# Reading the moving operand of TensorE products in turns of four columns from two halves, with another distance to the weight blocks

## The chip, the cores and the metric

The kernel runs on one core of a Trainium2 chip. The metric is the device time of one execution in microseconds. Engines are named as in the profile: PE (TensorE matmuls), PEld (its weight loads), DVE (VectorE), ACT (ScalarE), POOL (GpSimd) and SP, whose queue issues the DMAs.

## The reference

It is one inference step of a two-layer backbone with two groups of 128 tokens (context and latent), model width 2048. Both groups go through the same weights:

```python
for l in range(DEPTH):                                   # DEPTH = 2
    mod = silu(cond) @ w_ada[l] + b_ada[l]               # shift, scale, gate, twice
    h = rmsnorm(x, g_norm_mix[l]) * (1 + sc1) + sh1
    m = mixer_ab(h, ...) if l % 2 == 0 else mixer_c(h, ...)
    x = x + gt1 * m
    h = rmsnorm(x, g_norm_ffn[l]) * (1 + sc2) + sh2
    x = x + gt2 * conv_ffn(h, ...)                       # D_FF = 5632
y = rmsnorm(x, g_final)
```

The even layer's mixer holds multi-head latent attention and grouped-query attention; the odd layer's is differential attention. Each has one input projection, attention over the group's own keys (for the latent group also over 128 cached keys), and one output projection. `conv_ffn` projects up to 2 x 5632 features, convolves each over three neighbouring tokens, multiplies silu(gate) by the value and projects down. All inputs are float32. Context tensors (compressed keys and values) are outputs too.

## The kernel before

Activations lie transposed: 128 features on the partitions, tokens along the row, the 128 context tokens first and the 128 latent tokens behind them (NT = 256 columns). A product of an activation with a weight matrix runs over blocks of 128 x 128 weights. To get float32 accuracy from TensorE's faster type (fp32r), both sides are split into a high and a low part: `split` (L215 to L217) has ACT write the high part and DVE the difference. An operand tile thus holds, for each block of 128 features, 256 columns of high parts and 256 of low parts (ROW = 512 columns, 2,048 bytes): `hx` (normalised activations, also the attention output of the even layer), `g` (gated features), `oall` (attention output of the odd layer), `ql` (query latents), and `kv_in`, which has 3 x 128 columns, cached keys in the middle.

For each block, `gemm` (L300) issues three matmuls into one PSUM bank (tile `acc`): high weights with high operand (L309), high weights with low operand (L310), low weights with high operand (L313). Each matmul has its own weight load of 128 columns (512 bytes per partition). `first_three` (L279) does the same for the first three output blocks of a stage, interleaved (L295 to L297). Outputs are read from PSUM by ACT or DVE (residual add, convolution, copies), in token order.

Weights come by DMA from SP's queue, 1 MB at a time, into `raw` (3 buffers), and are split into `wh` and `wl` (4 buffers each, 1,024 columns, eight blocks of 512 bytes). The products of adaLN (`w_ada`) are worked in between: some on PE (L434, plain f32 with 32 weight columns), some on DVE (L419), paced by `pump` with rates per stage. Attention scores and values (L635, L649 to L651, L951, L970 to L972) and transposes (L382, L625, L876, L937, L992) are plain f32 matmuls.

The tile framework orders the instructions with a simulated timeline; only steps marked `keep_in_program_order` are pinned. Stages follow one another: even mixer (to about 497 us of the profile), ConvFFN of layer 0 (497 to 1205), odd mixer (1205 to 1690), ConvFFN of layer 1 (1690 to 2362), final norm.

Where a tile lies in a partition follows from the order of the pools. Small `pad` tiles set the addresses modulo 512: one in the weight pool (L112) and one ahead of the operands in each stage's pool (L659, L910, L1023), the latter sized by `SHIFT`. In the kernel before all operands of these products lie at 96 modulo 512 and all weight blocks at 160, so an operand starts 64 bytes ahead of a block in address (-64, which is SHIFT = 448, modulo 512).

Of the kernel before, what the change touches and what calls it, by code (L numbers as in the profile page):

```python
# [17 lines left out]
P = 128  # L18
D = 2048
KD = D // P  # L20
T = 128
NT = 2 * T
ROW = 2 * NT
SHIFT = 448
NL = 2
GRID_W = 64
EPS = 1e-6
# [56 lines left out]
def step_kernel(ctx: ExitStack, tc: tile.TileContext, A: dict):  # L84
    nc = tc.nc
    pe, dve, act, pool, sp = nc.tensor, nc.vector, nc.scalar, nc.gpsimd, nc.sync

    keep = ctx.enter_context(tc.tile_pool(name="keep", bufs=1))
    wpool = ctx.enter_context(tc.tile_pool(name="wpool", bufs=3))
# [13 lines left out]
    def nm(s):  # L103
        uid[0] += 1
        return f"{s}_{uid[0]}"

    def T_(pl, shape, tag, dt=F32, bufs=None):
        kw = {} if bufs is None else {"bufs": bufs}
        return pl.tile(shape, dt, tag=tag, name=nm(tag), **kw)


    T_(wpool, [P, 48], "pad", bufs=1)  # L112


    cst = T_(keep, [P, NCONST], "cst")
# [70 lines left out]
    def bank():  # L186
        return T_(pmisc, [P, 512], "misc")

    def att_bank():
        return T_(ppool["att"], [P, 512], "att", bufs=3)  # L190
# [30 lines left out]
    class Weights:  # L221
# [29 lines left out]
        def chunk(self):  # L251
# [24 lines left out]
            out, self.blocks = self.blocks[:self.nblk], self.blocks[self.nblk:]  # L276
            return out

    def first_three(W, xh, xl, order, mid=None, fixed=False):  # L279


        pin = tc.keep_in_program_order if fixed else lambda i: i
        raws = [W.load() for _ in range(3)]
        ps = [T_(pacc, [P, 512], "acc") for _ in range(3)]
        blocks = {(c, h): W.halves(raws[c], 8 * h) for c, h in ((0, 0), (1, 0), (2, 0), (0, 1))}
        count = [0] * 3
        for n, (c, k) in enumerate(order):
            if mid and n == len(order) // 2:
                mid()
            if (c, k // 8) not in blocks:  # L290
                blocks[c, k // 8] = W.halves(raws[c], 8)
            wh, wl = blocks[c, k // 8][k % 8]
            a, b = count[c] == 0, count[c] == KD - 1
            count[c] += 1
            pin(pe.matmul(ps[c][:, :NT], wh, xh(k), start=a, stop=False))  # L295
            pin(pe.matmul(ps[c][:, :NT], wh, xl(k), start=False, stop=False))  # L296
            pin(pe.matmul(ps[c][:, :NT], wl, xh(k), start=False, stop=b))  # L297
        return [p[:, :NT] for p in ps]

    def gemm(blocks, xh, xl, n=NT, first=0, between=None):  # L300


        fixed = lambda i: tc.keep_in_program_order(i) if between else i
        ps = T_(pacc, [P, 512], "acc")
        last = len(blocks) - 1
        for i in range(last + 1):
            k = (i + first) % (last + 1)
            wh, wl = blocks[k]
            fixed(pe.matmul(ps[:, :n], wh, xh(k), start=(i == 0), stop=False))  # L309
            fixed(pe.matmul(ps[:, :n], wh, xl(k), start=False, stop=False))  # L310
            if between and i == (last + 1) // 2:
                between()
            fixed(pe.matmul(ps[:, :n], wl, xh(k), start=False, stop=(i == last)))  # L313
        return ps[:, :n]


# [227 lines left out]
    def modulated(st, l, which, W, fixed):  # L544
# [29 lines left out]
        def turn():  # L574
            rest[1](tc.keep_in_program_order)

        ps = first_three(W, lambda k: hx[:, k, :NT], lambda k: hx[:, k, NT:2 * NT],
                         AS_MADE if fixed else IN_TURN, lambda: sum_rows(2, raws[2]), fixed)
        if fixed:
# [75 lines left out]
    def mixer_ab(hx, rb0, st):  # L655
        l = 0
        with tc.tile_pool(name="ab", bufs=1) as ab:
            with tc.tile_pool(name="abp", bufs=1) as pj:
                T_(ab, [P, SHIFT // 4], "pad")  # L659
                kv_in = T_(ab, [P, 4, 2, 3 * T], "kv_in", F32R)  # L660
# [104 lines left out]
                def part(W, k0, n, first, rate, between=None, **kw):  # L765

                    for c in range(23):
                        ps = gemm(W.chunk(), lambda k: hx[:, k0 + k, :NT], lambda k: hx[:, k0 + k, NT:2 * NT])
                        to = pr[:, c] if c < 15 else qb[:, c - 15]
                        if first:  # L770
                            act.copy(to, ps)
                        else:
                            dve.tensor_tensor(out=to, in0=to, in1=ps, op=ALU.add)
                        if between:
                            between(c)
                        pump(rate, **kw)
# [34 lines left out]
            with tc.tile_pool(name="abh", bufs=1) as hp:  # L811
# [35 lines left out]
                for h in range(8):  # L847
                    if h % 2 == 0:
                        for i in range(2):
                            ps = gemm(WQ.chunk(), qh, qlo)  # L850
                            qn[h + i] = T_(hp, [P, NT], "qn", bufs=4)
                            act.copy(qn[h + i], ps)
                            pump(RATE["heads"])
                        ps = gemm(WQ.chunk(), qh, qlo)
                        ev = T_(tmp, [P, NT], "nt", bufs=4)
                        act.copy(ev, ps)
                        qr = T_(hp, [P, NT], "qr", bufs=2)
                        act.copy(qr[:, 0:T], ev[:, 0:T])
                        rope(qr[:, None, T:], ev[:, None, T:], 1, 32, "rcm", "rsm")
                        pump(RATE["heads"])  # L860
# [34 lines left out]
    def mixer_c(cp, hx, W, ready, todo, st):  # L895
# [13 lines left out]
        product = lambda: ready.pop(0) if ready else gemm(W.chunk(), xh, xl, between=todo.pop(0) if todo else None)  # L909
        T_(cp, [P, SHIFT // 4 - 24], "pad")  # L910
        o_all = T_(cp, [P, KD, ROW], "oall", F32R)
# [90 lines left out]
        W = Weights(A["w_out_c"], KD, 1)  # L1002
        oh, ol = (lambda k: o_all[:, k, :NT]), (lambda k: o_all[:, k, NT:2 * NT])
        ready = first_three(W, oh, ol, LAST_LATE)
        for c in range(KD):
            fine[0] = c >= KD - QUIET[2]
# [8 lines left out]
    def ffn(hx, W, ready, todo, l, st):  # L1015
# [4 lines left out]
        with tc.tile_pool(name=f"ffn{l}", bufs=1) as fp, banks(f"pffn{l}") as pf:  # L1020
            feat["home"], feat["pool"] = fp, pf
            feat["due"] = 0.0
            T_(fp, [P, SHIFT // 4], "pad")  # L1023

# [53 lines left out]
    with banks("pab") as ppool["ada"]:  # L1078
# [4 lines left out]
        ps = [bank(), att_bank()]  # L1083
# [168 lines left out]
```

## Time and profile before

| what | value |
|---|---|
| median of two runs | 2388.72 us (2388.01 to 2389.42) |
| profiled execution, first to last instruction (its span) | 2384.0 us; no other time of it is recorded |
| left between span and median | 4.7 us |
| PE busy | 2333.9 us, 98% of the span |
| PEld busy | 2201.5 us, 92% |
| DVE busy | 1775.5 us, 74% |
| ACT busy | 1164.9 us, 49% |
| DMA | 612.94 MB, mean 257 GB/s |
| mean granted TensorE clock | 0.994 |

A matmul in the profile lasts longer than the distance to the next, because matmuls overlap in the array; the busy share of PE is not its pace. The pace is read from the starts, or from the number of matmuls in a stretch. In a group's line the columns are source line, engine, operation, output<-inputs, shapes and count, then busy time and mean duration of one, then the idle time ahead of them and what ended it.

### The profile page before, as it was taken

The numbers are of one execution on the slowest core, as the hardware profiler recorded it, in microseconds if no ns is written. First come the engines' busy times: TensorE is split into PE (matmuls) and PEld (weight loads), VectorE is DVE, ScalarE is ACT, GpSimd is POOL, SyncE is SP. The second block draws the span as 40 slices with busy tenths as digits, with TensorE's granted clock in tenths as the row PEclk, the third lists the DMA queues.
The fourth block names the chain that finished last, engine by engine and source line by source line (L and its number), as shares of the span: only waits on it lengthen the run. The fifth ranks groups of instructions, "written<-read, shape, count | busy, mean of one in ns | idle before, by whom it ended". The sixth has DMA issues, their size and how long they took to land. (4 is left out here: it accounts for less than half of the span.)

```text
span 2384.0 us, 47535 instructions
## 1 busy us (share of the span) xinstructions
PE 2333.9 (98%) x19784; PEld 2201.5 (92%) x19784; DVE 1775.5 (74%) x2720; ACT 1164.9 (49%) x1817; POOL 167.6 (7%) x205
## 2 busy tenths in 40 slices
PE   8999999999999999999999999999999999999997
PEld 6778868789999999999989999998999999999997
DVE  2667545569999999999979777878899855666654
ACT  4345544365554345554455444445655534555542
POOL 0001101100000000001220000023000000000011
PEclk9999999999999999999999999999999999999999
DMA  8886678877777876777766787776767655555553
GB/s 347 352 336 250 226 282 310 317 269 260 261 253 282 296 278 252 265 263 270 297 238 235 277 295 293 257 300 265 257 250 261 212 194 193 193 194 193 194 194 123
DMA packets 92551, 612.94 MB, mean 257 GB/s; under 512 B 9969, under 2 KB 17841, under 8 KB 20529
## 3 DMA queue, kind: packets, MB, share of 16 engines
q1 hardware_dynamic: 92336, 609.91, 69.7%
q8 instruction: 155, 2.54, 0.4%
q14 instruction: 60, 0.48, 0.1%
HBM read 605.12 MB, written 4.75 MB: 256 GB/s over the span
## 5 line engine op out<-in xcount | busy, mean ns | idle before, releaser
L216 ACT CAST wh<-raw 128x1024 fp32r<-128x1024 f32 (+1 forms) x788 | 793.7, 1013 | 963.8 <-PE acc L310 803.0
L217 DVE TENSOR_TENSOR wl<-raw,wh 128x1024 fp32r<-128x1024 f32 (+1 forms) x788 | 921.2, 1182 | 368.9 <-ACT wh L216 363.1
L309 PE MATMUL acc<-hx,wh 128*128 128x256 f32 x4064 | 1132.3, 279 | 10.9 <-ACT wh L216 4.2
L313 PE MATMUL acc<-hx,wl 128*128 128x256 f32 x4064 | 1129.1, 278 | 0.8 <-DVE wl L217 0.8
L310 PE MATMUL acc<-hx,wh 128*128 128x256 f32 x4064 | 1128.3, 278 | 0.0
L309 PEld LDWEIGHTS acc<-hx,wh 128*128 128x128 f32 x4064 | 764.4, 188 | 40.9 <-issue 16.3
L313 PEld LDWEIGHTS acc<-hx,wl 128*128 128x128 f32 x4064 | 764.3, 188 | 11.8 <-issue 8.7
L310 PEld LDWEIGHTS acc<-hx,wh 128*128 128x128 f32 x4064 | 764.9, 188 | 9.4 <-issue 7.9
L310 PE MATMUL acc<-g,wh 128*128 128x256 f32 x1408 | 388.3, 276 | 0.0
L313 PE MATMUL acc<-g,wl 128*128 128x256 f32 x1408 | 388.0, 276 | 0.0
L309 PE MATMUL acc<-g,wh 128*128 128x256 f32 x1408 | 387.8, 276 | 0.0
L419 DVE CUSTOM_DVE_ANT_0 junk<-araw,condb 128x2048 f32<-128x2048 f32 x120 | 274.6, 2289 | 0.0
L310 PEld LDWEIGHTS acc<-g,wh 128*128 128x128 f32 x1408 | 264.3, 188 | 0.0
L313 PEld LDWEIGHTS acc<-g,wl 128*128 128x128 f32 x1408 | 264.1, 188 | 0.0
L309 PEld LDWEIGHTS acc<-g,wh 128*128 128x128 f32 x1408 | 264.0, 188 | 0.0
L172 POOL TENSOR_TENSOR sqacc<-sqacc,sq 128x256 f32<-128x256 f32 x62 | 82.0, 1322 | 1521.7 <-issue 1216.1
L463 DVE SCALAR_TENSOR_TENSOR aacc<-araw,condw,aacc 128x512 f32<-128x512 f32 x150 | 111.3, 767 | 0.2
L586 DVE SCALAR_TENSOR_TENSOR x<-acc,mod,x 128x128 f32<-128x128 f32 x192 | 58.1, 343 | 56.0 <-PE acc L313 55.0
L1030 ACT ACTIVATE cv<-acc,convw 128x256 f32<-128x256 f32 x176 | 98.3, 558 | 1.4 <-PE acc L297 1.4
L434 PE MATMUL ada<-araw,condw 128*32 128x512 f32 x704 | 94.6, 614 | 3.8 <-DMA araw<-w_ada 3.0
L1036 DVE SCALAR_TENSOR_TENSOR cv<-acc,convw,cv 128x254 f32<-128x254 f32 x176 | 84.2, 479 | 3.5
L1033 DVE SCALAR_TENSOR_TENSOR cv<-acc,convw,cv 128x254 f32<-128x254 f32 x176 | 83.5, 475 | 2.6 <-ACT cv L1030 2.5
(236 smaller groups left out, 1893.0 us busy)
## 6 DMA issues: line engine op xcount, KB each, us to landing
araw<-w_ada SPq DMA_DIRECT2D x186, 1024.0 KB, 5.8
raw<-w_up SPq DMA_DIRECT2D x176, 1024.0 KB, 4.8
raw<-w_down SPq DMA_DIRECT2D x88, 1024.0 KB, 4.8
raw<-w_in_c SPq DMA_DIRECT2D x48, 1024.0 KB, 5.3
raw<-w_in_ab SPq DMA_DIRECT2D x19, 1024.0 KB, 7.0
raw<-w_out_ab SPq DMA_DIRECT2D x16, 1024.0 KB, 6.8
raw<-w_out_c SPq DMA_DIRECT2D x16, 1024.0 KB, 4.8
raw<-w_ada SPq DMA_DIRECT2D x6, 1024.0 KB, 9.9
```

The lines of the kernel that those rows point to most:

```text
L172: pool.tensor_tensor(out=st["acc"], in0=st["acc"], in1=sq, op=ALU.add)
L216: pin(act.copy(out_hi, src))
L217: pin(dve.tensor_tensor(out=out_lo, in0=src, in1=out_hi.bitcast(F32), op=ALU.subtract))
L309: fixed(pe.matmul(ps[:, :n], wh, xh(k), start=(i == 0), stop=False))
L310: fixed(pe.matmul(ps[:, :n], wh, xl(k), start=False, stop=False))
L313: fixed(pe.matmul(ps[:, :n], wl, xh(k), start=False, stop=(i == last)))
L419: tc.keep_in_program_order(dve.tensor_tensor_reduce(out=T_(feat["pool"], [P, D], "junk"), in1=feat["row"][:, c], in0=feat["raw"].rearrange ...
L434: i = pe.matmul(ada["ps"][32 * g:32 * g + 32, :], condw[:, 4 * t + g, :], raw[:, g], start=(t == 0), stop=(t == 3), skip_group_check=True)
L463: i = dve.scalar_tensor_tensor(out=acc[:, c], in0=raw[:, g], scalar=condw[:, k, c:c + 1], in1=acc[:, c], op0=ALU.mult, op1=ALU.add)
L1030: pin(act.activation(y, ps, AF.Identity, scale=cw[:, 1, m:m + 1], bias=cw[:, 3, m:m + 1]))
L1033: pin(dve.scalar_tensor_tensor(out=y3[:, :, 1:], in0=p3[:, :, :T - 1], scalar=cw[:, 0, m:m + 1], in1=y3[:, :, 1:], op0=ALU.mult, op1=ALU.add))
L1036: pin(dve.scalar_tensor_tensor(out=y3[:, :, :T - 1], in0=p3[:, :, 1:], scalar=cw[:, 2, m:m + 1], in1=y3[:, :, :T - 1], op0=ALU.mult, op1=A ...
```

## The change

Three edits. A helper `paired` gives a view of a row with 128 x j columns in which the order is: 4 columns of the first 128, 4 columns of the second 128, (4 of the third,) then the next 4 of the first, and so on. All products of `first_three` and `gemm` read their moving operand in that order and write their PSUM tile in the same order, so each result lands where it did. `SHIFT` becomes 256, and the pad in the weight pool grows from 48 to 96 columns: weight blocks move from 160 to 352 modulo 512, operands stay at 96, the distance becomes 256.

```diff
-SHIFT = 448
+SHIFT = 256
+RUN = 4
...
-    T_(wpool, [P, 48], "pad", bufs=1)
+    T_(wpool, [P, 96], "pad", bufs=1)
...
+    def paired(ap):
+
+        return ap.rearrange("p (j i e) -> p i j e", i=T // RUN, e=RUN)
...
-            pin(pe.matmul(ps[c][:, :NT], wh, xh(k), start=a, stop=False))
-            pin(pe.matmul(ps[c][:, :NT], wh, xl(k), start=False, stop=False))
-            pin(pe.matmul(ps[c][:, :NT], wl, xh(k), start=False, stop=b))
+            out = paired(ps[c][:, :NT])
+            pin(pe.matmul(out, wh, paired(xh(k)), start=a, stop=False))
+            pin(pe.matmul(out, wh, paired(xl(k)), start=False, stop=False))
+            pin(pe.matmul(out, wl, paired(xh(k)), start=False, stop=b))
...
         ps = T_(pacc, [P, 512], "acc")
+        out = paired(ps[:, :n])
...
-            fixed(pe.matmul(ps[:, :n], wh, xh(k), start=(i == 0), stop=False))
-            fixed(pe.matmul(ps[:, :n], wh, xl(k), start=False, stop=False))
+            fixed(pe.matmul(out, wh, paired(xh(k)), start=(i == 0), stop=False))
+            fixed(pe.matmul(out, wh, paired(xl(k)), start=False, stop=False))
             if between and i == (last + 1) // 2:
                 between()
-            fixed(pe.matmul(ps[:, :n], wl, xh(k), start=False, stop=(i == last)))
+            fixed(pe.matmul(out, wl, paired(xh(k)), start=False, stop=(i == last)))
```

## The prediction

> **What bounds the kernel now.** I read the page first (shares of the engines), then the stretches of the run by stage, then the groups of matmuls with their shapes, and last the timeline of single matmuls.
>
> ```profile
> span 2384.0 us, 47535 instructions
> PE 2333.9 (98%) x19784; PEld 2201.5 (92%) x19784; DVE 1775.5 (74%) x2720; ACT 1164.9 (49%) x1817; POOL 167.6 (7%) x205
> ```
>
> ```profile
> 380.00:497.00 117.00, 114.65 (x937) 93.33 (x936) 63.67 (x119) 50.49 (x88) 24.01 (x23) 0.99 0.87 330
> 497.00:1205.00 708.00, 705.51 (x6222) 704.38 (x6222) 641.63 (x806) 355.03 (x465) 24.85 (x14) 1.00 0.73 268
> 1690.00:2362.00 672.00, 672.00 (x5932) 672.00 (x5931) 468.59 (x614) 332.69 (x437) 15.68 (x13) 1.00 0.58 206
> ```
>
> The columns of the second view are the stretch in us, its length, busy time of PE, of its weight loads, of DVE, ACT and POOL, the granted clock, DMA share and GB/s. Both ConvFFN stages (497 to 1205 and 1690 to 2362) are TensorE from end to end at clock 1.00. Nobody keeps PE waiting there, so what counts is the time from one matmul to the next. A busy PE is pipelined (each lasts longer than the step to the next), so the step is read from starts and counts:
>
> ```profile
> 600.00:1200.00 600.00, 600.00 (x5297) 600.00 (x5296) 552.89 (x689) 292.58 (x383) 24.64 (x14) 1.00 0.74 272
> 1700.00:2300.00 600.00, 600.00 (x5297) 600.00 (x5296) 428.28 (x558) 298.65 (x388) 6.73 (x5) 1.00 0.60 212
> ```
>
> 600 us / 5297 = 113.3 ns per product of 256 columns, equal in both, though DVE is at 92% in one and 71% in the other, and DMA at 0.74 and 0.60. The step therefore belongs to PE and what it reads, not to its neighbours. Each product has its own weight load of 128 columns, and it starts with the product ahead:
>
> ```profile
> 699.81 0.28 PE L309 MATMUL acc<-hx,wh 128*128 128x256 f32 x1
> 700.49 0.28 PE L309 MATMUL acc<-hx,wh 128*128 128x256 f32 x1
> ```
> ```profile
> 699.81 0.19 PEld L310 LDWEIGHTS acc<-hx,wh 128*128 128x128 f32 x1
> ```
>
> Is 113.3 ns the least that 256 columns take? Three rows say no. The first pair stands 149 steps apart in the odd layer's mixer. The next pair is the plain f32 product of `attend`: 256 columns, two records per instruction. Then four transposes in a row on the chain of waits, 128 columns each.
>
> ```profile
> 1417.13 0.28 PE L309 MATMUL acc<-hx,wh 128*128 128x256 f32 x1
> 1434.68 0.28 PE L313 MATMUL acc<-hx,wl 128*128 128x256 f32 x1
> ...
> 1438.31 0.60 PE L970 MATMUL att<-dv,pT 128*128 128x256 f32 x2
> 1438.74 0.59 PE L971 MATMUL att<-dv,pT 128*128 128x256 f32 x2
> ```
> ```profile
> 1675.91 0.44 PE misc L382 x4
> 1676.34 0.12 PE acc L313
> ```
>
> (1434.68 - 1417.13) / 149 = 117.8 ns: the same instruction with the same addresses modulo 512 runs at a **second pace**, for 150 products on end, at clock 1.00. Counted over the trace, of 17,637 steps from a 256-column product 15,760 last 113 to 115 ns, 1,550 last 116 to 120, and none is under 113. The f32 product takes 0.43 us for two records, 215 ns each, and a transpose 108 to 110 (0.43 us to the next start and 0.44 us, over 4). A column of such a record costs twice one of an fp32r product (215 / 256 against 113.3 / 256), so a transpose has the array time of a 256-column fp32r product, the same 128-column weight load beside it, and comes out faster; half an f32 record of 256 columns is 107.5. So the least is about 108 to 109 ns, the usual pace is 4.3 ns above 109, the second pace 4.4 ns above that. Products of 384 columns agree:
>
> ```profile
> 234.85 0.34 PE L309 MATMUL acc<-kv_in,wh 128*128 128x384 f32 x1
> 235.71 0.34 PE L313 MATMUL acc<-kv_in,wl 128*128 128x384 f32 x1
> ```
>
> Five steps in 0.86 us: 172 ns, against 1.5 x 108.5 = 163.
>
> My reading: two equal steps of 4.4 ns that come and stay, under unchanged addresses, are a meeting of two streams, counted once or twice per product. The moving operand walks 1,024 bytes of a partition while the weight load walks 512, so modulo 512 one laps the other once per product; with the start 64 bytes behind, one meeting is early, and whether a second fits in depends on the time between the two starts. In a transpose both streams walk 512 bytes in the same time and nothing is lost.
>
> **The change part by part.** It removes and adds no instruction: stripped of line numbers and shapes, the order on all five engines and queues is unchanged, so no wait, DMA or buffer moves. Three things differ.
>
> 1. *Addresses.* Weight blocks move from 160 to 352 modulo 512; operands stay at 96. The distance goes from -64 to 256. By itself this may move products between the two paces: alone it would be worth 0 to +4.4 ns each.
>
> 2. *Order of the columns.* Each product takes 4 columns (16 bytes) from one half of its row, then 4 from the other, 512 bytes on. Modulo 512 the moving operand now advances 16 bytes per 8 columns, 512 bytes per product, as fast as the weights. At equal pace a distance of 256 stays 256, so the streams never meet: the case of the transposes. For 384 columns the operand advances slower than the weights (16 bytes per 12 columns), 512 x 2/3 = 341 bytes while the weights walk 512, so the distance shrinks by 171 from 256 and still doesn't close.
>
> 3. *Turns.* 64 turns per product read and write in runs of four. No row of this trace shows a split operand on PE. From below: nothing, since a contiguous row passes 64 borders of 16 bytes too inside its 113.3 ns. From above: starting a stream anew. Two transposes cost 2 x 110 = 220 against 215 for one f32 record of 256 columns, so a start costs at most 5 ns; 63 more of them are 315 ns per product. I take the value from below, as the contiguous row is the nearest; a rival holds the other.
>
> Sum, against the profiled execution. Products by group (one of three equal lines each):
>
> ```profile
> L309 PE MATMUL acc<-hx,wh 128*128 128x256 f32 x4064 | 1132.3, 279 | 10.9 <-ACT wh L216 4.2 <-ACT hx L537 2.5 <-ACT cv L1030 2.5
> L309 PE MATMUL acc<-g,wh 128*128 128x256 f32 x1408 | 387.8, 276 | 0.0
> L309 PE MATMUL acc<-oall,wh 128*128 128x256 f32 x208 | 57.9, 279 | 0.0
> L296 PE MATMUL acc<-hx,wh 128*128 128x256 f32 x144 | 41.4, 293 | 3.1 <-POOL hx L522 2.7
> L309 PE MATMUL acc<-kv_in,wh 128*128 128x384 f32 x64 | 22.7, 355 | 0.0
> L309 PE MATMUL acc<-ql,wh 128*128 128x256 f32 x72 | 20.8, 288 | 0.0
> L296 PE MATMUL acc<-oall,wh 128*128 128x256 f32 x48 | 14.0, 293 | 0.0
> ```
>
> Without kv_in: 3 x (4064 + 1408 + 208 + 144 + 72 + 48) = 17,832 products of 256 columns, and 192 of 384. Of these the two ConvFFNs have 2 x 3 x (88 x 16 + 32 x 22) = 12,672.
> - ConvFFNs: 12,672 x 4.3 ns = 54.5 us.
> - Other 256-column products: 5,160 x 4.3 = 22.2 us.
> - Second pace: 1,550 x 4.4 = 6.8 us.
> - 384 columns: 192 x 9 = 1.7 us.
>
> Together 85 us. Off this comes what lies beside the path. Up to 497 us DMA is at 0.83 to 0.92 of its engines and PE has gaps; some 2,300 products there are worth 10 us and I take half. DVE is the next engine to be late:
>
> ```profile
> 740.00:850.00 110.00, 110.00 (x973) 110.00 (x973) 103.59 (x120) 43.28 (x41) 0.00 (x0) 1.00 0.77 287
> ```
>
> In this down projection it has 103.59 us of work in 110; PE would want 110 x 109 / 113.3 = 105.8, so the cover just holds, at 98%; 2 us off for queueing. If it failed, the stretch would fall to 103.6 at best, so no gain is lost beyond those microseconds. DMA would need 287 x 1.04 = 298 GB/s there, and 330 is reached from 380 to 497. Net gain 85 - 5 - 2 = 78 us: span 2384.0 - 78 = 2306. The median of the runs shown, 2388.72, lies 4.7 above this span, so **2311 us**. Bounds of the pace are 107.5 (half the f32 record) and 111 (about half of the way back to 113.3): 18,024 x (-1.5 to +2) = -27 to +36 us, so 2284 to 2347; I cut the low end to 2288, as the stages ahead of 497 follow only in part.
>
> **The rivals.**
>
> *A. The change doesn't do what it says: nothing met, and the pace stays.* Then 4.3 ns belong to the form, the rounded product of 256 columns, and turns cost nothing: 2389, anything within 2345 to 2436. For it: none of 17,637 steps is under 113. Against it: the second pace, which the form cannot explain. [...]
>
> *B. Turns cost time.* Each run of four is a fresh place in the operand and in the result. One column time, (215 - 110) / 256 = 0.41 ns, per turn gives 64 x 0.41 = 26 ns; less the 4.3 gained, 22 ns x 18,024 = 396 us: 2785. It decides from 4.3 / 64 = 0.07 ns per turn on; below that the change still gains. For it: no row shows PE at such a pattern. Against it: 16 bytes borders are passed in every row already. [...]
>
> *C. Equal pace makes a meeting last.* If the true distance (start of the load, its own delay, direction of its walk) isn't 256, streams of equal pace don't pass each other but stay together, or a walk in the other direction meets twice. At the second pace throughout: 16,300 x 4.4 = 72 us more: 2461; a lasting meeting costs more. For it: the weight load's real reading time isn't in the trace. Against it: the load starts with the product to within the 10 ns that the rows above resolve, worth under 50 bytes of the 256, and the transposes, at other distances, run at 108 to 110.
>
> **How the numbers follow.** Forecast (2288 to 2347) 0.61, A 0.14, B 0.14, C 0.11. The likeliest gives 2311. For the range, forecast and A together hold 0.75; taking in C up to the second pace throughout makes 0.81: 2288 to 2465. B lies outside. What a measurement of this kernel can tell from no change is 2%, 48 us: faster means below 2341. Almost the whole forecast is faster (0.59); the rest of it and A are the same (0.16); B and C are slower (0.25).
>
> **What would show it.** Right: 5,500 PE records in each of the two 600 us stretches above, in place of 5,297 (600 / 109); a mean near 272 in the hx and g groups in place of 276 to 279; no stretch at 117 to 118; kv_in steps near 163; transposes and `attend` as before; DVE near 98% in the first down projection. A shows as 5,297 again; B as one single, longer pace in all groups, 384 columns at 1.5 times it, and DVE idle; C as a pace of 117 or more with two values. The prediction is wrong if turns aren't free, which no row here can exclude, or if the meeting isn't where the 4.3 ns come from.

## The result, and the profile after

The changed kernel takes 2617.23 us (2616.9 to 2617.55, two runs) against 2388.72: ratio 1.0955, 95% interval 1.0923 to 1.0986. It is slower by 9.6%, on the side of rivals B and C and outside the range of the forecast.

The page of the changed kernel, and its stretches (length; busy time of PE, PEld, DVE, ACT, POOL; clock; DMA share; GB/s):

```profile
span 2614.8 us, 47527 instructions
PE 2566.9 (98%) x19784; PEld 2434.6 (93%) x19784; DVE 1788.0 (68%) x2720; ACT 1178.8 (45%) x1817; POOL 158.8 (6%) x205
```
```profile
600.00:1200.00 600.00, 600.00 (x4740) 600.00 (x4739) 499.89 (x623) 270.05 (x349) 0.00 (x0) 1.00 0.66 240
1900.00:2500.00 600.00, 600.00 (x4739) 600.00 (x4739) 379.39 (x494) 267.75 (x346) 2.53 (x2) 1.00 0.52 186
780.00:890.00 110.00, 110.00 (x870) 110.00 (x870) 90.85 (x106) 40.24 (x40) 0.00 (x0) 1.00 0.70 259
```

The number of matmuls is the same, 19,784, and in the ConvFFNs PE still never waits. But 600 us hold 4,740 products where they held 5,297: 600 / 4740 = 126.6 ns for each, in place of 113.3, in the first stretch and in the last alike. All groups of products are longer (the records of the first hx group 295 ns after 279, of the first kv_in group 377 after 355), and the plain f32 transposes, whose lines the change doesn't touch, are not: 275 after 274 (the last line below is that of the kernel before):

```profile
L316 PE MATMUL acc<-hx,wh 128*128 128x256 f32 x4064 | 1197.3, 295 | 11.6 <-ACT wh L217 5.1 <-ACT hx L544 2.5 <-ACT cv L1037 2.3
L316 PE MATMUL acc<-kv_in,wh 128*128 128x384 f32 x64 | 24.1, 377 | 0.0
L389 PE MATMUL ada<-cst,am 128*128 128x128 f32 x102 | 16.1, 275 | 1.8 <-ACT am L382 1.8
```
```profile
L382 PE MATMUL ada<-cst,am 128*128 128x128 f32 x102 | 16.1, 274 | 1.5 <-ACT am L375 1.5
```

The sum comes out close. 12,672 products of the ConvFFNs and 3,610 others lose 13.3 ns each, the 1,550 that had the second pace lose 8.8, and 192 products of 384 columns lose 19 (their median step is 193 ns after 174): 217 + 14 + 4 = 235 us, against 230.8 us between the two spans. Nothing else moved: DVE has the same 1.8 ms of work and is at 83% (90.85 of 110 us, third stretch) in the down projection, which now runs from 783 to 917 us; the forecast had it at 98% there.

So the time went into the matmuls, evenly in the ConvFFNs. In the mixers the changed kernel has two paces, as the kernel before has. Between these two rows of the odd mixer lie 108 steps:

```profile
1390.78 0.29 PE L316 MATMUL acc<-hx,wh 128*128 128x256 f32 x1
1404.70 0.29 PE L316 MATMUL acc<-hx,wh 128*128 128x256 f32 x1
```

13.92 us / 108 = 128.9 ns. Some 1,250 steps of the trace last 128 to 130 ns, nearly all of them in the mixers; most of the others last 126 or 127. The sum above has them at 126.6, so they add about 3 us to it.

What remains is which part of the change did it: the new distance to the weight blocks, the order of reading, or the order of writing; and whether a turn has a price of its own.

### The profile page after: what moved, and what is told of

Same layout as the page of the kernel before. It is cut to its first block, busy times and chain, and to the rows that moved or that the text cites. A ratio compares the mean times of both kernels' runs of the same rounds, so it can differ in the third digit from the quotient of the medians.

```text
span 2614.8 us, 47527 instructions
## 1 busy us (share of the span) xinstructions
PE 2566.9 (98%) x19784; PEld 2434.6 (93%) x19784; DVE 1788.0 (68%) x2720; ACT 1178.8 (45%) x1817; POOL 158.8 (6%) x205
## 4 chain that ended last, share of the span: by engine, by line
PE 95%; DVE 2%; issue 1%; DMA 1%; ACT 1%; POOL 0%; POOLq 0%; DVEq 0%; ACTq 0%
PE acc L316 28%; PE acc L320 28%; PE acc L317 28%; PE ada L441 3%; PE acc L302 1%; PE att L642 1%; PE acc L301 1%; PE acc L303 1%; DMA raw<-w_in_ab 0%; PE att L958 0%; DVE nt L540 0%; PE ada L389 0%; PE att L632 0%; DVE nt L534 0%; PE misc L441 0%
## 5 line engine op out<-in xcount | busy, mean ns | idle before, releaser
L217 ACT CAST wh<-raw 128x1024 fp32r<-128x1024 f32 (+1 forms) x788 | 809.9, 1033 | 1182.0 <-PE acc L317 990.1
L316 PE MATMUL acc<-hx,wh 128*128 128x256 f32 x4064 | 1197.3, 295 | 11.6 <-ACT wh L217 5.1
L320 PE MATMUL acc<-hx,wl 128*128 128x256 f32 x4064 | 1194.5, 294 | 0.4 <-DVE wl L218 0.2
L317 PE MATMUL acc<-hx,wh 128*128 128x256 f32 x4064 | 1193.8, 294 | 0.0
L317 PE MATMUL acc<-g,wh 128*128 128x256 f32 x1408 | 411.6, 293 | 0.0
L320 PE MATMUL acc<-g,wl 128*128 128x256 f32 x1408 | 411.3, 293 | 0.0
L316 PE MATMUL acc<-g,wh 128*128 128x256 f32 x1408 | 411.2, 293 | 0.0
```

Of the source, the lines that this page charges most:

```text
L217: pin(act.copy(out_hi, src))
L316: fixed(pe.matmul(out, wh, paired(xh(k)), start=(i == 0), stop=False))
L317: fixed(pe.matmul(out, wh, paired(xl(k)), start=False, stop=False))
L320: fixed(pe.matmul(out, wl, paired(xh(k)), start=False, stop=(i == last)))
```

## The experiments

Steps below are from the start of one product to the start of the next. Times of single runs stand beside a run of the kernel before on the same chip.

### The parts one by one

Four kernels undo parts of the change. The first keeps the addresses and takes the order away (`paired` returns its argument):

```diff
     def paired(ap):
-        return ap.rearrange("p (j i e) -> p i j e", i=T // RUN, e=RUN)
+        return ap
```

> Only the addresses change: weight blocks at 256 from the operands, columns read and written in plain order. The step of a 256-column product is 113.3 ns in the kernel before and 126.6 ns in the changed one. If the addresses alone made the 13.3 ns (a contiguous reader also loses by the distance): 126 ns, about 2617 us. If a contiguous reader laps the weights once or twice whatever the distance: 113 to 118 ns, 2389 to 2461 us. If it meets them less often at 256: 109 ns, 2311 us.

Measured: 2491.29 us beside 2383.89. The second keeps the order and restores the pads (48 columns in the weight pool, `SHIFT` = 448):

> Only the order changes: turns of four read and written, distance left at -64. Theory turns (each of the 64 turns costs 0.27 ns, wherever the blocks lie): 126.6 ns again, about 2617 us. Theory distance (two streams of equal pace stay at a bad distance): another distance gives another price, 109 ns (2311 us) or well over 127 ns (over 2650 us).

Measured: 2613.41 us. The third and the fourth split reading from writing; both leave the tokens of a product in another order, so that the rest of the step works on mixed tokens with the same amount of work:

```diff
+    def written(ap):
+
+        return ap
...
-            out = paired(ps[c][:, :NT])
+            out = written(ps[c][:, :NT])
...
-        out = paired(ps[:, :n])
+        out = written(ps[:, :n])
```

> Distance 256, operand read in turns of four, result written in plain order, so that the tokens of each product stand in another order and what follows works on mixed tokens; the amount of work is the same. Turns cost on reading, or the locked distance does: 126.6 ns, about 2617 us. Turns cost on writing PSUM alone: the step falls to 109 to 113 ns, 2311 to 2389 us.

Measured: 2617.56 us. The fourth has the old pads again and swaps the two helpers' work:

```diff
     def paired(ap):
 
-        return ap.rearrange("p (j i e) -> p i j e", i=T // RUN, e=RUN)
+        return ap
+
+    def written(ap):
+
+        return ap.rearrange("p (j i e) -> p i j e", i=T // 4, e=4)
```

> Kernel before with its result alone written in turns of four (tokens mixed as in the run that reads so; same amount of work), read in plain order, distance -64. Turns cost on writing: 113.3 + 13 to 18 ns, 2620 to 2710 us. Turns cost on reading or the locked distance does: 113.3 ns, 2389 us.

Measured: 2389.24 us beside 2383.89. The same 500 us of the first ConvFFN in the kernel before and in the four kernels, in this order (before, addresses alone, order alone, reading alone, writing alone):

```profile
600.00:1100.00 500.00, 500.00 (x4415) 500.00 (x4414) 460.49 (x581) 248.30 (x322) 0.00 (x0) 1.00 0.74 270
```
```profile
600.00:1100.00 500.00, 500.00 (x4169) 500.00 (x4168) 441.03 (x552) 232.20 (x303) 0.00 (x0) 1.00 0.69 254
```
```profile
600.00:1100.00 500.00, 500.00 (x3950) 500.00 (x3949) 419.45 (x520) 223.81 (x286) 0.00 (x0) 1.00 0.66 240
```
```profile
600.00:1100.00 500.00, 500.00 (x3949) 500.00 (x3949) 419.40 (x522) 222.13 (x285) 0.00 (x0) 1.00 0.66 240
```
```profile
600.00:1100.00 500.00, 500.00 (x4414) 500.00 (x4414) 460.46 (x580) 247.92 (x323) 0.00 (x0) 1.00 0.73 270
```

Divide 500 us by the count: 113.3, 119.9, 126.6, 126.6 and 113.3 ns. Four things follow.

- **Reading in turns is the cost.** Alone at the old distance it gives 126.6 ns; with plain writing at the new distance too. In the ConvFFNs the distance of the changed kernel therefore plays no part in its pace. In the mixers the stretches at 128.9 ns appear only at distance 256 (the changed kernel and `read_turns`), not with the order alone; at some 2.2 ns for each of some 1,250 products they are worth about 3 us, an estimate.
- **Writing in turns of four is free**: 113.3 ns, as before.
- **The distance matters for plain reading**: 119.9 ns at 256 against 113.3 at -64, 107 us for the addresses alone. Without the turns this part of the change would have cost 4.5%.
- **The two costs don't add up.** The addresses alone cost 6.6 ns, the turns alone 13.3, both together 13.3.

### The price of a turn, measured by itself

One kernel is the kernel before with rows of 40 equal products behind its own work. Operand and weights are tiles of their own at addresses 0 modulo 512 from each other; each row has its own reading pattern and distance `d`:

```diff
+        for kind, d, wc in BENCH:
+            ps = bps.tile([P, 512], F32, tag="bp", name=f"{kind}_d{d}w{wc}z")
+            for r in range(40):
+                ...
+                tc.keep_in_program_order(pe.matmul(out, wts[:, w:w + wc], moving(kind, o), start=True, stop=True))
```

> The kernel before, and behind its own work rows of 40 equal products of 256 columns each, fp32r, with a weight load of 128 columns (some of 32) from other blocks: plain reading at sixteen distances; turns of four at eight distances; turns of 8, 16, 32 and 64; turns of four between two places whose spacing is 16, 64, 128, 256, 448, 512, 576, 640, 768 or 1,024 bytes; each column read twice; 128 columns read twice over; and pieces of these with 32 weight columns. Theory turns: every reading in turns of four costs 126 ns whatever distance, spacing and weight load, turns of 8 some 118, of 16 some 113. Theory spacing: the two lines of a turn, 512 bytes apart, get in each other's way; other spacings fall to 109 to 113 ns, and 32 weight columns change nothing. Theory weights: the cost comes from the weight load beside it; with 32 weight columns turns of four and plain reading both take about 109 ns. Meetings as in the prediction: plain reading has 113 ns near a distance of -64 and 118 to 120 elsewhere, and a column read twice (equal pace, no turns) has 109.

Its timeline shows rows of 40 products with their length (start, us, line, operation, name, shapes). `plain` is contiguous; the first `turn` row is turns of four; `twice` takes each of 128 columns two times in a row; `again` takes 128 columns and then the same 128 once more; `inner` takes every second column of eight, then the four left out; the first `gap` row takes turns of four between two places 16 bytes apart; `d` is the distance, `w` the number of weight columns:

```profile
2428.21 5.05 PE L1172 MATMUL plain_d256w128z<-bops,bwts 128*128 128x256 f32 x40
...
2458.55 4.82 PE L1172 MATMUL plain_d448w128z<-bops,bwts 128*128 128x256 f32 x40
...
2490.15 5.42 PE L1172 MATMUL turn_d256w128z<-bops,bwts 128*128 128x256 f32 x40
...
2506.53 5.33 PE L1172 MATMUL turn_d448w128z<-bops,bwts 128*128 128x256 f32 x40
...
2519.03 7.06 PE L1172 MATMUL inner_d256w128z<-bops,bwts 128*128 128x256 f32 x40
...
2594.67 4.73 PE L1172 MATMUL gap_d64w128z<-bops,bwts 128*128 128x256 f32 x40
...
2752.83 4.73 PE L1172 MATMUL twice_d64w128z<-bops,bwts 128*128 128x256 f32 x40
2757.62 4.73 PE L1172 MATMUL twice_d256w128z<-bops,bwts 128*128 128x256 f32 x40
2762.41 4.73 PE L1172 MATMUL twice_d448w128z<-bops,bwts 128*128 128x256 f32 x40
2767.20 4.98 PE L1172 MATMUL again_d64w128z<-bops,bwts 128*128 128x256 f32 x40
...
2777.35 4.82 PE L1172 MATMUL again_d448w128z<-bops,bwts 128*128 128x256 f32 x40
2782.22 4.90 PE L1172 MATMUL plain_d256w32z<-bops,bwts 128*32 128x256 f32 x40
```

A row's length holds its first products, which start unevenly; the steps below are means over products 8 to 40, read from the starts. The very first row (plain, distance 0) is left out: its first products are 213 ns apart, in a stretch with a mean granted clock of 0.65.

| reading of 256 columns, 128 weight columns | step, ns |
|---|---|
| plain, distance 192 or 448 | 113.3 |
| plain, distance 64 / 128 / 256 / 320 / 384 | 117.8 / 118.5 / 119.9 / 117.8 / 118.5 |
| plain, distance 32 / 96 / 160 / 224 | 116.7 / 120.0 / 117.3 / 118.3 |
| turns of 4, halves 512 bytes apart, eight distances | 126.7 to 129.5 |
| turns of 8 (three distances) | 123.3 |
| turns of 16 | 120.0 |
| turns of 32 | 118.8 to 119.2 |
| turns of 64, distance 64 / 256 / 448 | 117.8 / 120.0 / 113.3, as plain |
| turns of 4, places 16 bytes apart, three distances | 111.7 |
| turns of 4, places 64 or 576 bytes apart | 120.0 to 120.9 |
| turns of 4, places 128 or 640 bytes apart | 122.7 to 123.3 |
| turns of 4, places 256, 768 or 1,024 bytes apart | 126.7 |
| turns of 4, places 448 bytes apart, distance 64 / 256 / 448 | 122.3 / 120.0 / 123.3 |
| turns of 4 from four places 256 bytes apart | 134.8 to 138.8 |
| each column twice (512 bytes in all), three distances | 111.7 |
| 128 columns twice over, distance 64 / 256 / 448 | 117.8 / 120.0 / 113.3, as plain |
| every second column of eight, then the others, three distances | 170.0 |

With 32 weight columns at distance 256: plain 117.8, turns of four 124.5, places 16 bytes apart 109.2, each column twice 109.2, every second column 170.0.

None of the three theories comes out whole. For the theory of turns: every spacing from 64 bytes up keeps the pace at 120 ns or more, and cutting the weight load to a quarter takes only some 4 ns off the turns at this distance (128.8 to 124.5 ns). Against it: with places 16 bytes apart the reader takes turns all the same and has 111.7 ns. There the second four of each turn are the first four of the next, so that the reader goes back by four columns at most and gets through 132 columns in all, much as when it takes each column twice. Nor is the price fixed. It depends on the spacing of the two places, with the same values at 64 and 576, at 128 and 640, at 256, 768 and 1,024 bytes, and 512, the spacing of the two halves, is among the worst. It also doesn't halve with the number of turns: half the turns (of 8) keep 10 of the 13.3 ns.

The rows fall in order of another count, too: how often the reader goes on to another 16 bytes (four columns). Each column twice and places 16 bytes apart go through 32 and 33 such pieces and take 111.7 ns; plain reading and 128 columns twice over go through 64 and take 113.3 to 120; every second column changes piece 128 times and takes 170. No run varies this count alone, so it is a reading that fits and not one that is shown. The turns of the changed kernel cost more than plain reading at the same count of 64 (126.6 ns against 113.3 to 120).

One caution: the turns of four at 256 have 128.8 ns here, close to the second pace of the changed kernel's mixers (128.9), and 126.6 in its ConvFFNs. A row may thus stand in one of two paces.

A second kernel is the changed one with turns of 16 for reading and writing:

```diff
-        return ap.rearrange("p (j i e) -> p i j e", i=T // RUN, e=RUN)
+        return ap.rearrange("p (j i e) -> p i j e", i=T // 16, e=16)
```

> The changed kernel with turns of 16 columns in place of 4, distance 256. Theory turns (a fixed price per turn): a quarter of the 17.6 ns above 109, so about 113 ns and 2390 us. If what counts is the distance alone, as in plain reading at 256: 120 ns, about 2491 us.

Measured: 2494.56 us beside 2386.97, and the same count as with the addresses alone:

```profile
600.00:1100.00 500.00, 500.00 (x4169) 500.00 (x4168) 441.85 (x550) 232.19 (x304) 0.00 (x0) 1.00 0.70 255
```

119.9 ns. The forecast of 113 by a fixed price per turn failed; at distance 256, 16 turns of 16 are no dearer than plain reading.

### Is there a better place for plain reading?

> The kernel before with further rows of 40 products behind it: plain reading at distances from 400 to 496 in steps of 8 bytes and around 192; plain reading with 32 weight columns at eight distances, and with 64 at three; plain reading at 448 with the result written in runs of 4 and of 2 columns, 512 bytes apart; turns of four with spacings of 32, 480, 512 and 544 bytes; and turns with 32 weight columns. If the pace of plain reading is a matter of the distance modulo 256, the best place is one narrow dip at 448 and 192 of 113.3 ns or a little less; a place under 112 ns would give a kernel faster than the one before (18 us per ns). If the weight load is what plain reading meets, 32 weight columns flatten the sweep towards 109 ns; if the reader meets itself, the sweep stays at 113 to 120. Writing in runs of 4: 113.3 ns as in plain order; in runs of 2: the same if only whole 8-byte pieces count, more if every new place in PSUM costs. Turns of four with 32 weight columns: 123 to 125 ns again if the turn is paid by the reader alone.

The kernel is built as the one with rows above, with other rows; its first, at distance 400, is left out for the same reason. Its timeline around the distance of the kernel before; `flat` means written in plain order, `far` in runs of 4 and of 2 columns whose next run lies 512 bytes on:

```profile
2413.98 5.07 PE L1196 MATMUL plain_d440w128f_flatz<-bops,bwts 128*128 128x256 f32 x40
2419.10 4.82 PE L1196 MATMUL plain_d448w128f_flatz<-bops,bwts 128*128 128x256 f32 x40
2423.98 5.07 PE L1196 MATMUL plain_d456w128f_flatz<-bops,bwts 128*128 128x256 f32 x40
...
2474.65 4.73 PE L1196 MATMUL plain_d64w32f_flatz<-bops,bwts 128*32 128x256 f32 x40
...
2503.73 4.74 PE L1196 MATMUL plain_d448w32f_flatz<-bops,bwts 128*32 128x256 f32 x40
...
2513.47 4.77 PE L1196 MATMUL plain_d256w64f_flatz<-bops,bwts 128*64 128x256 f32 x40
2518.30 4.97 PE L1196 MATMUL plain_d448w64f_flatz<-bops,bwts 128*64 128x256 f32 x40
2523.32 4.80 PE L1196 MATMUL plain_d448w128f_far4z<-bops,bwts 128*128 128x256 f32 x40
2528.18 4.98 PE L1196 MATMUL plain_d448w128f_far2z<-bops,bwts 128*128 128x256 f32 x40
```

The good place is one point: 120.0 ns at 440, 113.3 at 448, 119.9 at 456; the same around 192 (120.0, 113.3, 119.9 at 184, 192, 200). No plain row of either kernel averaged less than 113.3, with 128, 64 or 32 weight columns; with 32 the distances 64, 192, 320 and 448 all give 113.3, 0 and 256 give 117.8, 128 and 384 give 115.5. With 64 weight columns the places change: 113.3 ns at 256, which is bad with 128 columns, and 119.1 at 448, which is good with them (116.7 at 64). So the weight load does take part in the 3 to 8 ns between a good and a bad distance, and which distance is good depends on its length, but the last 4 ns above 109 didn't go away with a quarter of the load. No distance was found that beats the kernel before.

Of the write patterns, runs of 4 take 113.3 ns and runs of 2 take 117.8. Turns of four with 32 weight columns gave 126.5 and 126.6 ns at 64 and 448, against 126.7 and 126.8 with 128: at these two distances the length of the weight load plays no part in the price.

Turns of four with places 32 bytes apart take 120.0 ns, 480 bytes apart 120.0 and 121.3, 544 bytes apart 124.5 and 123.3 (distances 64 and 448). 544 is 32 and 512 more, yet it costs 3 to 5 ns more, so not every spacing has the same price again 512 bytes further, as 64 and 128 have.

### The form of the pattern

Two more kernels have the old distance and longer turns (of 64 and of 8 columns, for reading and writing).

> The changed order with turns of 64 columns, two pairs per product, distance -64 as in the kernel before. If the three-step form of the pattern costs anything by itself: over 2389 us, up to 2613 us as with turns of four. If only the number of jumps between places counts (3 here against 63): 113.3 ns and 2384 to 2394 us, as in the row of equal products.

> The same with turns of 8 columns, 32 of them, distance -64. A fixed price per jump (13.3 ns for 63) gives 113.3 + 6.5 = 120 ns and about 2505 us. The row of equal products gave 123.3 ns: 113.3 + 10, about 2565 us; then the price of a jump isn't fixed, and half the jumps keep three quarters of the loss.

Measured: 2385.33 and 2551.11 us beside 2386.19.

```profile
600.00:1100.00 500.00, 500.00 (x4414) 500.00 (x4413) 460.54 (x581) 248.34 (x322) 0.00 (x0) 1.00 0.74 270
```
```profile
600.00:1100.00 500.00, 500.00 (x4056) 500.00 (x4055) 429.86 (x535) 225.55 (x293) 0.00 (x0) 1.00 0.68 249
```

113.3 ns with turns of 64: a pattern of three steps costs nothing as such, and the other order of columns neither. 123.3 ns with turns of 8: with the spacing of 512 bytes the loss grows with the number of jumps, but not in proportion: 10 / 31 = 0.32 ns a jump for 31 jumps, 13.3 / 63 = 0.21 ns for 63.

Both distances together suggest how the loss is made up. With turns of 64, 16, 8 and 4 the products take 113.3, 120.0, 123.3 and 126.6 ns at -64, and 120.0, 119.9, 123.3 and 126.6 at 256 (ConvFFNs, and rows where no kernel was run). From turns of 16 down the distance no longer matters: at -64 about half of the 13.3 ns is the good distance lost, which plain reading at 256 loses too, and the rest comes on top of 120 ns. This split is by the sizes alone; no run shows why.

## Why the prediction was wrong

**What bounds the kernel.** Right: the pace of PE, and nothing beside it. The whole difference is the step of one product times their number.

**The reading of the 113.3 ns.** Wrong. The prediction took the 4.3 ns above 109 for one meeting of two streams per product and the second pace for a second one. What the runs showed: the distance between operand and weights does move the pace (113.3 ns at 448, 120.0 at 440), and the length of the weight load moves the good place (with 64 weight columns 113.3 ns at 256 and 119.1 at 448). So the weight load bears on the pace; that two streams meet, and where, was the author's model, and no run shows it. The pattern repeats every 256 bytes, not every 512 as in that model (192 and 448, 64 and 320, 128 and 384 agree within 0.1 ns), the good place is under 16 bytes wide, and no distance gave less than 113.3. The 4.3 ns are the lowest price found for 256 columns read straight on, which is how rival A read them; its free turns were wrong.

**Step 1, addresses alone,** was put at 0 to +4.4 ns per product. It measured +6.6 ns, 107 us: mis-sized, since it was sized by the second pace, and the distance 256 is among the worst for plain reading.

**Step 2, equal pace and so 109 ns,** is not borne out. When each column is read twice, the operand walks 512 bytes as the weights do, and the pace is 111.7 ns at all three distances, where plain reading has 113.3 to 120. But such a row also reads half the bytes, and with 32 weight columns, where the paces aren't equal, it is faster still (109.2 ns). So it stays open whether the equal pace or the fewer bytes free it from the distance. The turns have the equal pace too, and their rows at eight distances still lie between 126.7 and 129.5 ns. The transposes on which this step leaned (108 to 110 ns) read 512 bytes without jumps back; the change buys the equal pace with 63 jumps.

**Step 3, turns at no price, is the step that failed.** The prediction bounded it from nothing to 315 ns per product and took nothing, because a contiguous row passes 64 borders of 16 bytes too. A border passed in order is not a jump to another place: the 63 jumps of the change cost 13.3 ns per product above plain reading at the old distance and 17.6 above the 109 ns of the forecast. In place of a gain of 78 us came a loss of 230.8 us of span. Rival B had the side and, in the ConvFFNs, the signs (one longer pace; elsewhere 384 columns at 193 / 126.6 = 1.5 times it); its price per turn, 0.41 ns, was half again too high (17.6 / 64 = 0.28), so where it said 2785 us the runs gave 2617. Half of B was wrong too: it named operand and result, and the result costs nothing (113.3 ns with the writing alone in turns); nor is there one price for any fresh place (111.7 ns with places 16 bytes apart, 126.7 at 256).

**Rival C** falls as the cause of the loss. In the ConvFFNs the pace is 126.6 ns at 256 and at -64; a lasting meeting would have changed with the distance. Its sign, two values of the pace, did show in the mixers (126.7 and 128.9 ns), but at 256 alone and for some 3 us.

**The weights' address, and runs in PSUM.** With the weight blocks 192 bytes further and the operands where they were, the same instructions take 119.9 ns in place of 113.3 (`addr_only`): the time changes with the address of the weights alone. Written jumps of 512 bytes after every 16 bytes cost nothing here (113.3 ns), after every 8 bytes some 4.5 ns (117.8).

**Not settled:** what makes a spacing of 256 bytes the dearest (126.7 ns), and what starts the second pace, of the kernel before and of the changed one. In both it comes in the mixers, where other matmuls stand between the products; in the rows of equal products no plain row at 448 with 128 weight columns took it (113.3 ns). The addresses alone have no second pace: 120.0 ns in mixers and ConvFFNs alike.

## What to carry to other kernels

When an operand is read in a new pattern, price the pattern itself before the collision it is meant to avoid: a row of 40 equal products behind the kernel's own work shows it in one run. Keep the moving operand of a matmul contiguous (113.3 ns here, against 126.6 in turns of four, both at the old distance); if it must alternate between two places, make the runs long (64 columns cost nothing here, 16 up to 7 ns, 4 some 13 at the old distance), and avoid places 256, 512, 768 or 1,024 bytes apart, the dearest spacings of two places that were measured (126.7 ns, and 126.7 to 129.5 at 512). And when two parts of a change belong together, run each alone: here the address part alone was a loss of 4.5% hidden under the larger one.

## What the runs showed that was not expected

- Plain reading has a good distance to the weight blocks that is one point wide: 8 bytes to either side cost 6.6 ns of 113.3, which over 17,832 products would be 118 us, an estimate; a distance of 256, with the same 6.6 ns, cost 107 us. With 64 weight columns the good place lies elsewhere (113.3 ns at 256, 119.1 at 448).
- The cost of alternating between two places depends on their spacing: 111.7 ns at 16 bytes, 120 at 64, 123 at 128, 126.7 at 256. The prices at 64 and 128 came again 512 bytes further, that at 256 at 768 and 1,024; the price at 32 (120) didn't come again at 544 (123 to 125).
- Reading every second column of eight, then the others, takes 170.0 ns, at three distances with 128 weight columns and at one with 32.
- PSUM takes runs of four columns, 512 bytes apart, at 113.3 ns, as in plain order.
